# Decoder layer on one core: two weight sums by adding transfers, four pairs in six gate blocks, and seven products for the last 1024 columns

## The chip, the cores and the metric

The kernel runs on one core of one Trainium2 chip. The metric is the device time of one execution in microseconds. Before the change the median of 3 runs is 1021.54 us (1021.4 to 1021.66).

## What is computed

One layer for 256 tokens of width 2048 in float32: a wide input projection, two token mixers (attention and a short gated convolution), two gates computed from the input, and an output projection.

```python
h = _rmsnorm(x, pre_norm_g)
proj = jnp.einsum('bsd,de->bse', h, w_in)
...
attn = attn.reshape(b, s, MLA_WIDTH) * jax.nn.silu(z_mla)
y_mla = jnp.einsum('bse,ed->bsd', attn, w_o_mla)
u = c_gate * c_in
...
y_conv = jnp.einsum('bse,ed->bsd', b_gate * conv * jax.nn.silu(z_conv), w_o_conv)
merged = jax.nn.sigmoid(g_mla) * y_mla + jax.nn.sigmoid(g_conv) * y_conv
out = jnp.einsum('bsd,de->bse', merged, w_out)
x = x + _rmsnorm(out, post_norm_g)
```

The change concerns the products with 2048 x 1024 pieces of `w_in` (z_conv, b_gate, g_mla, g_conv) and of `w_out`.

## The kernel before

**Split numbers.** Every float32 operand becomes two parts of a shorter format, high and low. For a weight, ACT writes the high part (`whi`, a copy that rounds) and DVE subtracts it from the original (`wlo`). One `product` (L90 is its matmul) is then three matmuls of a 128x128 stationary tile of tokens with 512 weight columns: high by high, high by low, low by high.

**Units.** Weights come in 192 units, numbered in load order, most of them 128x2048 floats (1 MiB). `load_raw` issues each on the queue of SP into one of three `raw` buffers; `split_unit` makes `whi` and `wlo` in rings of three. `take(i)` calls `ahead`, which writes the loads three units and the splits one unit further down the program than the matmuls that use them. Matmuls are kept in program order, as is what is marked `keep_in_program_order`; a scheduler places the rest, each engine runs its own list in order, and semaphores join the lists.

**Blocks.** From about 419 us on the kernel works through eight gate blocks (`block(n, ...)`, 1024 columns each: units 81 to 88, 89 to 96, and so on to 137 to 144), then 32 units of two square products (the stage `sq`, 145 to 176), then a block with the first 1024 columns of the output projection (177 to 184, named `OUT`), then its last 1024 columns as eight units (185 to 192). A block has eight units of 256 input rows and fills eight PSUM banks. A **whole** unit gives 24 matmuls to the banks 2, 3, 4, 0. A **pair** is a unit whose two row groups and two column halves are multiplied as a 2x2 matrix product with seven products instead of eight (21 matmuls), into the banks 7, 5, 1, 6, 4, 2, 3 in this order. It needs sums of the token tiles, made once by `token_sums` (`xs`), and sums of the four column blocks of the unit: `split_pair` makes them on DVE in three steps, blocks 1 and 2 less block 0 into `tf` (1024 columns), one into block 0's place in `raw`, one into `tf`; then the parts `thi` (ACT) and `tlo` (DVE). `tf`, `thi` and `tlo` exist once. `PLACES` says which units of a block are pairs: 2 and 4 in block 0, 0, 2 and 4 in the blocks 1 to 7, 3 and 5 in `OUT`; the rest are whole.

**The end of a block.** After its last pair ACT copies bank 1 to `p1` and DVE makes three sums `u` from the banks 6, 7 and 5; that frees the banks 1, 6, 7, 5 for the next block. Behind the last unit `done` adds one of `p1`, `u` to each of the banks 2, 3, 4, 0. For gates the sum goes to a tile `sg` and through a sigmoid, and POOL's queue stores it to memory; stage `sq` loads it again. For the output, `out_block` squares the result on ACT, multiplies it by the norm's gain into `og`, and `finish` scales it, adds the residual `xr` and stores it.

**The last columns.** The third 512 columns (four units) go through the bank pair `cv`; of the last 512 the four units' parts are kept, so that the first half of the tokens is through and being normalised while the second half is multiplied. `xr`, 2 MB, is loaded on ACT's queue when that stage begins.

Of the kernel before, what the change touches and what calls it, by code (L numbers as in the profile page):

```python
# [84 lines left out]
def tile_layer(ctx: ExitStack, tc: tile.TileContext, xw, x, pos, pvec, post_g, wc, wz, wcv, wkr, wqk, wqr, wv, cwr, wsq, wg, out):  # L85
# [61 lines left out]

    u_g.append([add(wg[OUT, i], kind=kinds[OUT][i][0]) for i in range(KD // 2)])
    u_out = {(c, k): add(wsq[2, c, k], kind="whole") for c in (2, 3) for k in range(4)}

    raws, splits, early = {}, {}, {}
    done = {"raw": 0, "split": 0}

    def load_raw(i):
        ap, w, _ = plan[i]
# [3 lines left out]
        cuts = {0: (S, XW, 2 * XW), 1: (0, XW, 2 * XW), 2: (0, XW, 2 * XW)}.get(i, (0, w))  # L159
# [10 lines left out]
    def split_unit(i):  # L170
# [28 lines left out]
        for h in range(0, w, n):  # L199
            e = min(h + n, w)  # L200
            split_act(hi[:, h:e], lo[:, h:e], t[:, h:e])
        splits[i] = hi, lo

    tpool = {}

    def split_pair(i, t, hi, lo):

        raw = t[:, :].rearrange("p (b c) -> p b c", b=4)
        tf = tpool["f"].tile([P, 2, 3, S], F32, name=f"tf{i}", tag="tf", bufs=1)[:, :, :, :].rearrange("p a b c -> p (a b c)")
        tf = tf.rearrange("p (b c) -> p b c", b=3)  # L210
        thi, tlo = (tpool["t"].tile([P, 3, 512], F32R, name=f"t{o}{i}", tag=f"t{o}", bufs=1) for o in ("hi", "lo"))
# [4 lines left out]
        nc.scalar.activation(hi[:, 512:], t[:, 512:], AF.Copy)  # L216
        tt(tf[:, :2], raw[:, 1:3], raw[:, 0:1].to_broadcast([P, 2, 512]), op=ALU.subtract)
        tt(raw[:, 0], raw[:, 2], tf[:, 0], op=ALU.add)
        tt(tf[:, 2], raw[:, 3], raw[:, 0], op=ALU.subtract)
        nc.scalar.activation(hi[:, :512], t[:, :512], AF.Copy)  # L220
        nc.scalar.activation(thi[:, :, :], tf[:, :, :], AF.Copy)  # L221
# [93 lines left out]
    at_f = fp.tile([P, H, S], F32, name="at_f")  # L315
    cv_f = fp.tile([P, KD, S], F32, name="cv_f")
# [469 lines left out]
    def token_sums(pool, pairs):  # L786
# [14 lines left out]
        tt(a22, a21, a22, op=ALU.add)  # L801
# [3 lines left out]
        tt(a12, a12, a11, op=ALU.subtract)  # L805
# [31 lines left out]
    for h in range(H):  # L837
# [21 lines left out]
        if h == H - 3:  # L859
            lstack.close()  # L860
            tpool["f"] = dstack.enter_context(tc.tile_pool(name="d0", bufs=1))
            sums = token_sums(tpool["f"], PAIRS)
            next(sums)
# [42 lines left out]
    def side(n, j):  # L906

        i = {5: 0, 6: 1, 7: 2, 3: 3}.get(n)
        if i is not None:
            return [tpool["xs"][:, i, j, h] for h in range(2)]  # L910
# [8 lines left out]
    def block(n, done, jobs):  # L919
# [42 lines left out]
        for m, t, half, other in ((2, 0, 0, p1[:, :]), (3, 0, 1, u[:, 0]), (4, 1, 0, u[:, 2]), (0, 1, 1, u[:, 1])):  # L962
            done(ps[m][:, :], other, t, half)

# [3 lines left out]
    def open_spool():  # L968
        bstack.close()
        spool["pool"] = main.enter_context(tc.tile_pool(name="sp", bufs=1, side="right"))  # L970
        spool["pool"].tile([P, 512], F32, name="sg_first", tag="sg", bufs=4)
        spool["w"] = wstack.enter_context(tc.tile_pool(name="cw", bufs=1, side="right")).tile([P, NT, D], F32, name="cv_w")
# [12 lines left out]
    gate_far = {}  # L985

    def g_done(n, b):
        def done(ps, other, t, half):
            c = 2 * b + half
            g = spool["pool"].tile([P, 512], F32, name=f"sg{n}{c}{t}", tag="sg", bufs=4)  # L990
            nc.vector.tensor_tensor(g[:, :], ps, other, op=ALU.add)
# [305 lines left out]
```

## Time and profile before

| what | value |
|---|---|
| median of 3 runs | 1021.54 us |
| profiled execution | 1021.4 us |
| its span in the trace | 1019.6 us |
| gate blocks, from the first to the last matmul | 419 to 752 us |
| stage `sq` | 752 to 926 us |
| block `OUT` | 926 to 968 us |
| last 1024 columns | 968 to 1011.7 us |
| traffic to and from memory | 240.46 MB, mean 236 GB/s |
| matmuls in the program | 4608 |

The span runs from the first to the last instruction of the trace; 1.8 us of the profiled execution lie around it. PE is the matrix engine and PEld its loading of stationary tiles, DVE and ACT the two engines that split, POOL and SP issue transfers. The four stages of the table are told apart by the names of the tiles that the matmuls write and read.

### The profile page before, as it was taken

The numbers are of one execution on the slowest core, as the hardware profiler recorded it, in microseconds if no ns is written. First come the engines' busy times: TensorE is split into PE (matmuls) and PEld (weight loads), VectorE is DVE, ScalarE is ACT, GpSimd is POOL, SyncE is SP. The second block draws the span as 40 slices with busy tenths as digits, with TensorE's granted clock in tenths as the row PEclk, the third lists the DMA queues.
The fourth block names the chain that finished last, engine by engine and source line by source line (L and its number), as shares of the span: only waits on it lengthen the run. The fifth ranks groups of instructions, "written<-read, shape, count | busy, mean of one in ns | idle before, by whom it ended". The sixth has DMA issues, their size and how long they took to land.

```text
span 1019.6 us, 12601 instructions
## 1 busy us (share of the span) xinstructions
PE 1010.1 (99%) x4619; PEld 842.3 (83%) x4619; DVE 798.5 (78%) x1010; ACT 547.0 (54%) x682; POOL 199.8 (20%) x381
## 2 busy tenths in 40 slices
PE   9999999999999999999999999999999999999996
PEld 7888888888888888888888888888888888888885
DVE  7578787887869777888989889898878875678762
ACT  7756555565566664655545456555653443344551
POOL 7530311232213223200000000000024431322000
PEclk9999999999999999999999999999999999999999
DMA  8755785786666656665566566665679896778662
GB/s 324 301 193 195 229 258 184 216 282 234 218 225 219 244 191 232 218 221 212 176 223 237 213 236 240 213 247 216 238 254 329 312 338 216 267 257 283 214 242 82
DMA packets 44830, 240.46 MB, mean 236 GB/s; under 512 B 8096, under 2 KB 8800, under 8 KB 21856
## 3 DMA queue, kind: packets, MB, share of 16 engines
q1 hardware_dynamic: 29808, 197.54, 54.6%
q0 software_dynamic: 14528, 38.82, 11.7%
q10 hardware_dynamic: 432, 3.29, 0.9%
q8 instruction: 36, 0.59, 0.2%
q14 instruction: 26, 0.21, 0.1%
HBM read 217.63 MB, written 17.83 MB: 231 GB/s over the span
## 4 chain that ended last, share of the span: by engine, by line
PE 98%; DMA 1%; DVE 0%; ACT 0%; SPq 0%; DVEq 0%; issue 0%
PE g L90 37%; PE cv L90 26%; PE sq L90 17%; PE out L90 4%; PE kn L90 2%; PE qn L90 2%; PE vv L90 2%; PE ckv L90 2%; PE qa L90 2%; PE sc L90 1%; PE qr L90 1%; PE o L90 1%; DMA raw<-xw_dram 1%; PE kr L90 0%; DVE og L1149 0%; SPq L161 0%
## 5 line engine op out<-in xcount | busy, mean ns | idle before, releaser
L273 DVE TENSOR_TENSOR wlo<-raw,whi 128x1024 fp32r<-128x1024 f32 (+2 forms) x233 | 363.7, 1578 | 124.5 <-ACT whi L272 123.6
L272 ACT ACTIVATE whi<-raw 128x1024 fp32r<-128x1024 f32 (+2 forms) x235 | 307.2, 1334 | 251.7 <-PE sq L90 85.2
L90 PE MATMUL g<-whi,x_both 128*128 128x512 f32 x852 | 275.0, 389 | 0.0
L90 PE MATMUL cv<-whi,x_both 128*128 128x512 f32 x768 | 242.9, 390 | 0.0
L90 PEld LDWEIGHTS g<-whi,x_both 128*128 128x128 f32 x852 | 159.9, 188 | 33.3
L90 PEld LDWEIGHTS cv<-whi,x_both 128*128 128x128 f32 x768 | 144.2, 188 | 29.3
L90 PE MATMUL g<-wlo,x_both 128*128 128x512 f32 x426 | 165.7, 389 | 0.0
L90 PE MATMUL cv<-wlo,x_both 128*128 128x512 f32 x384 | 149.7, 390 | 0.0
L359 POOL DMA_DIRECT2D far<-via x96 | 52.6, 554 | 231.1 <-DVE via L352 229.2
L90 PEld LDWEIGHTS g<-wlo,x_both 128*128 128x128 f32 x426 | 80.0, 188 | 16.5
L90 PEld LDWEIGHTS cv<-wlo,x_both 128*128 128x128 f32 x384 | 72.2, 188 | 13.9
L216 ACT ACTIVATE whi<-raw 128x1536 fp32r<-128x1536 f32 x25 | 37.3, 1491 | 80.1 <-PE g L90 49.3
L90 PE MATMUL sq<-whi,x_both 128*128 128x512 f32 x256 | 79.0, 389 | 0.0
L90 PE MATMUL sq<-whi,cv_both 128*128 128x512 f32 x256 | 79.0, 389 | 0.0
L214 DVE TENSOR_TENSOR wlo<-raw,whi 128x2048 fp32r<-128x2048 f32 x25 | 57.2, 2290 | 8.1 <-ACT whi L220 8.1
L90 PEld LDWEIGHTS sq<-whi,x_both 128*128 128x128 f32 x256 | 48.0, 188 | 9.9
L90 PEld LDWEIGHTS sq<-whi,cv_both 128*128 128x128 f32 x256 | 48.0, 188 | 9.9
L90 PE MATMUL sq<-wlo,x_both 128*128 128x512 f32 x128 | 49.8, 389 | 0.0
L90 PE MATMUL sq<-wlo,cv_both 128*128 128x512 f32 x128 | 49.8, 389 | 0.0
L214 DVE TENSOR_TENSOR tf<-raw 128x1024 f32<-128x1024 f32 (+1 forms) x50 | 47.7, 954 | 0.8
L214 DVE TENSOR_TENSOR tlo<-tf,thi 128x1536 fp32r<-128x1536 f32 x25 | 43.8, 1753 | 2.3 <-ACT thi L221 2.3
L221 ACT ACTIVATE thi<-tf 128x1536 fp32r<-128x1536 f32 x25 | 37.1, 1484 | 10.7 <-PE g L90 9.3
(248 smaller groups left out, 1389.9 us busy)
## 6 DMA issues: line engine op xcount, KB each, us to landing
raw<-wg_dram SPq DMA_DIRECT2D x72, 1024.0 KB, 4.8
raw<-wsq_dram SPq DMA_DIRECT2D x40, 1024.0 KB, 6.1
raw<-wcv_dram SPq DMA_DIRECT2D x32, 1024.0 KB, 4.9
raw<-wz_dram SPq DMA_DIRECT2D x16, 1024.0 KB, 4.9
raw<-wqk_dram SPq DMA_DIRECT2D x8, 1024.0 KB, 5.1
raw<-wc_dram SPq DMA_DIRECT2D x4, 1024.0 KB, 10.0
raw<-wv_dram SPq DMA_DIRECT2D x4, 1024.0 KB, 4.8
gate<-sg POOLq DMA_DIRECT2D x16, 256.0 KB, 2.6
```

Of the source, the lines that this page charges most:

```text
L90: return tc.keep_in_program_order(nc.tensor.matmul(*a, **kw))
L214: tc.keep_in_program_order(nc.vector.tensor_tensor(*a, op=op))
L216: nc.scalar.activation(hi[:, 512:], t[:, 512:], AF.Copy)
L221: nc.scalar.activation(thi[:, :, :], tf[:, :, :], AF.Copy)
L272: a = nc.scalar.activation(hi, src, AF.Copy)
L273: b = nc.vector.tensor_tensor(lo, src, hi.bitcast(F32), op=ALU.subtract)
L359: tc.keep_in_program_order(nc.gpsimd.dma_start(out=f[i], in_=m))
```

## The change

1. **Sums by addition.** The two differences in `split_pair` become sums; the signs move into `token_sums` and into the last steps of `u`.
2. **Two sums by transfer.** For the pairs from unit 93 to the end of block 7 the first two sums no longer run on DVE. A transfer on POOL's queue writes column block 0 into two places of `tf`, and a second one, with an adding write, adds the blocks 1 and 2. The unit's own load leaves out its first 512 columns, which DVE then fills with the third sum as before.
3. **Doubled buffers.** `tf`, `thi` and `tlo` alternate between two places (the pools `d0` and `d2`; the second `tf` lies in the place of `u`).
4. **Four pairs** (units 0, 2, 4, 6) in the blocks 1 to 6. `extra_sums`, in block 1, makes the token sums of the fourth. One whole unit is left behind the last pair instead of three. `u` and `p1` lie in the four `sg` tiles, the gates are made in place, and their stores go to SP's queue, at the third unit of the next block (`store`). `ahead(..., split=2)` at a block's last pair and last unit brings splits one unit further forward.
5. **The last 1024 columns as a block** (`OUT + 1`) with pairs at the units 1 and 3. Its last three units are kept (`KEPT`) and used bank by bank (`last_units`); the sum for the last bank is split into two parts (`more`) and added by two matmuls with an identity matrix (`one`). `out_block` of `OUT` moves to the third unit of this block, and `xr` goes into the place of `cv_f`, which is free earlier.

The program has 4586 matmuls.

```diff
-    u_g.append([add(wg[OUT, i], kind=kinds[OUT][i][0]) for i in range(KD // 2)])
-    u_out = {(c, k): add(wsq[2, c, k], kind="whole") for c in (2, 3) for k in range(4)}
+    u_g += [[add(wg[n, i], kind=kinds[n][i][0]) for i in range(KD // 2)] for n in (OUT, OUT + 1)]
+    FIRST_SUM = u_g[1][4]
...
-        ap, w, _ = plan[i]
+        ap, w, kind = plan[i]
+        by_dma = kind == "pair" and FIRST_SUM <= i <= u_g[OUT - 1][-1]
+        if by_dma:
+            sums_by_dma(i, ap)
...
-        cuts = {0: (S, XW, 2 * XW), 1: (0, XW, 2 * XW), 2: (0, XW, 2 * XW)}.get(i, (0, w))
+        cuts = {0: (S, XW, 2 * XW), 1: (0, XW, 2 * XW), 2: (0, XW, 2 * XW)}.get(i, (512 if by_dma else 0, w))
...
-        if u_out[3, 0] <= i < u_out[3, 3]:
-            hi, lo = (op2.tile([P, UNIT], F32R, name=f"w{o}{i}") for o in ("hi", "lo"))
+        if i == u_g[-1][-1]:
+            both = fp.tile([P, 2, UNIT], F32R, name="w_kept", tag="at_f", bufs=1)
+            hi, lo = both[:, 0], both[:, 1]
...
+    def sum_tile(i):
+        second = "t2" in tpool and tpool["n"] % 2
+        tpool["n"] += 1
+        if second:
+            return tpool["t"].tile([P, 3, 512], F32, name=f"tf{i}", tag="u", bufs=1)[:, :, :], True
+        tf = tpool["f"].tile([P, 2, 3, S], F32, name=f"tf{i}", tag="tf", bufs=1)[:, :, :, :].rearrange("p a b c -> p (a b c)")
+        return tf.rearrange("p (b c) -> p b c", b=3), False
+    def sums_by_dma(i, ap):
+        tf, _ = sums_come[i] = sum_tile(i)
+        keep = tc.keep_in_program_order
+        keep(nc.gpsimd.dma_start(out=tf[:, :2], in_=ap[:, :512].rearrange("p (a c) -> p a c", a=1).to_broadcast([P, 2, 512])))
+        keep(nc.gpsimd.dma_start(out=tf[:, :2], in_=ap[:, 512:1536].rearrange("p (a c) -> p a c", a=2), accum_op=ALU.add))
...
-        tf = tpool["f"].tile([P, 2, 3, S], F32, name=f"tf{i}", tag="tf", bufs=1)[:, :, :, :].rearrange("p a b c -> p (a b c)")
-        tf = tf.rearrange("p (b c) -> p b c", b=3)
-        thi, tlo = (tpool["t"].tile([P, 3, 512], F32R, name=f"t{o}{i}", tag=f"t{o}", bufs=1) for o in ("hi", "lo"))
+        tf, second = sums_come.get(i) or sum_tile(i)
+        thi, tlo = (tpool["t2" if second else "t"].tile([P, 3, 512], F32R, name=f"t{o}{i}", tag=f"t{o}", bufs=1) for o in ("hi", "lo"))
...
+        if i not in sums_come:
+            tt(tf[:, :2], raw[:, 1:3], raw[:, 0:1].to_broadcast([P, 2, 512]), op=ALU.add)
         tt(raw[:, 0], raw[:, 2], tf[:, 0], op=ALU.add)
-        tt(tf[:, 2], raw[:, 3], raw[:, 0], op=ALU.subtract)
-        nc.scalar.activation(hi[:, :512], t[:, :512], AF.Copy)
-        nc.scalar.activation(thi[:, :, :], tf[:, :, :], AF.Copy)
+        tt(tf[:, 2], raw[:, 3], raw[:, 0], op=ALU.add)
+        rounded(hi[:, :512], t[:, :512])
+        rounded(thi[:, :, :], tf[:, :, :])
...
-        tt(a22, a21, a22, op=ALU.add)
+        tt(a22, a21, a22, op=ALU.subtract)
         tt(a21, a11, a21, op=ALU.subtract)
         yield
         tt(a11, a22, a11, op=ALU.subtract)
-        tt(a12, a12, a11, op=ALU.subtract)
+        tt(a12, a12, a11, op=ALU.add)
...
+            if i == len(kinds) - kept:
+                return last_units(ps, units[i:], kinds[i:], w, u, p1)
...
-                p1 = wide("p1")
-                u = tpool["t"].tile([P, 3, 512], F32, name="u", tag="u", bufs=1)
-                nc.scalar.activation(p1[:, :], ps[1][:, :], AF.Copy)
-                tt = nc.vector.tensor_tensor
-                tt(u[:, 0], ps[6][:, :], p1[:, :], op=ALU.add)
-                tt(u[:, 2], ps[7][:, :], u[:, 0], op=ALU.add)
+                if i > 5:
+                    ahead(units[i], split=2)
+                if 0 < n < OUT:
+                    p1, *u = (spool["pool"].tile([P, 512], F32, name=f"u{n}{o}", tag="sg", bufs=4)[:, :] for o in range(4))
+                else:
+                    p1, u = wide("p1")[:, :], tpool["t"].tile([P, 3, 512], F32, name="u", tag="u", bufs=1)
+                    u = [u[:, o] for o in range(3)]
+                nc.scalar.activation(p1, ps[1][:, :], AF.Copy)
+                def tt(*a, op):
+                    r = nc.vector.tensor_tensor(*a, op=op)
+                    if last_pair > 5:
+                        tc.keep_in_program_order(r)
+                tt(u[0], ps[6][:, :], p1, op=ALU.add)
+                tt(u[2], ps[7][:, :], u[0], op=ALU.add)
                 for o in (1, 0):
-                    tt(u[:, o], u[:, 2 * o], ps[5][:, :], op=ALU.subtract)
+                    tt(u[o], ps[5][:, :], u[2 * o], op=ALU.subtract)
+        if n < OUT - 1:
+            ahead(units[-1], split=2)
+        for m, t, half, other in ((2, 0, 0, p1), (3, 0, 1, u[0]), (4, 1, 0, u[2]), (0, 1, 1, u[1])):
             done(ps[m][:, :], other, t, half)
+    def last_units(ps, units, kinds, w, u, p1):
+        ws = [w]
+        pool = out_tiles["pool"]
+        one, more = pool.tile([P, P], F32R, name="one"), pool.tile([P, 2, 512], F32R, name="more")
+        nc.scalar.activation(one[:, :], ident[:, :], AF.Copy)
+        for t, banks in enumerate((((2, p1), (3, u[0])), ((4, u[2]), (0, u[1])))):
+            for half, (m, other) in enumerate(banks):
+                if m == 0:
+                    for a in range(2):
+                        matmul(ps[m][:, :], one[:, :], more[:, a], start=False, stop=False)
+                for i, (_, ks) in enumerate(kinds):
+                    if i == len(ws):
+                        ws.append(take(units[i]))
+                    for j, k in enumerate(ks):
+                        a = [x_both[:, k, o + t * P : o + (t + 1) * P] for o in (0, S)]
+                        product(ps[m][:, :], a, ws[i](2 * j + half, 512), False, i == len(kinds) - 1 and j == 1)
+                if t == 0 == half:
+                    split_act(more[:, 0], more[:, 1], u[1], True)
+                out = ps[m][:, :]
+                if t == 0 or half == 0:
+                    nc.vector.tensor_tensor(other, out, other, op=ALU.add)
+                    out = other
+                rr = out_block(2 + half, t, out)
+            finish(t, rr)
+    def extra_sums():
+        hi = tpool["t2"].tile([P, 4, P], F32R, name="xs4hi")
+        lo = tpool["t"].tile([P, 512], F32R, name="xs4lo", tag="p1", bufs=1)[:, :].rearrange("p (i t) -> p i t", i=4)
+        xf = spool["pool"].tile([P, 512], F32, name="xf4", tag="sg", bufs=4)[:, :].rearrange("p (g s) -> p g s", g=2)
+        tpool["xs4"] = hi, lo
...
+            tt(xf[:, g], a[:, 3 + STEP * g, :S], a[:, 3 + STEP * g, S:], op=ALU.add)
+        (a11, a21), (a12, a22) = [[xf[:, g, t * P : (t + 1) * P] for t in range(NT)] for g in range(2)]
+        tt(a22, a21, a22, op=ALU.subtract)
+        tt(a21, a11, a21, op=ALU.subtract)
+        tt(a11, a22, a11, op=ALU.subtract)
+        tt(a12, a12, a11, op=ALU.add)
+        for i, f in enumerate((a22, a11, a21, a12)):
+            split_act(hi[:, i], lo[:, i], f, True)
...
+    def store():
+        while stores:
+            stores.pop(0)()
...
-            tc.keep_in_program_order(nc.gpsimd.dma_start(out=gate_far[n, c, t][:, :], in_=g[:, :]))
+            far = gate_far[n, c, t]
+            stores.append(lambda: nc.sync.dma_start(out=far[:, :], in_=g))
...
+        jobs = {2: [extra_sums]} if n == 0 else {2: [store]}
+    store()
     split_branch(3)
...
+        out_later.append(lambda: out_block(half, t, other))
...
-    block(OUT, out_done, {3: [open_out]})
-    main.close()
-    op2 = ctx.enter_context(tc.tile_pool(name="op2", bufs=1))
-    xr, og = op2.tile([P, NT, D], F32, name="xr"), out_tiles["og"]
-    nc.scalar.dma_start(out=xr[:, :, :], in_=x)
-    pss = [bank(f"out2_{t}", tag="cv", bufs=2) for t in range(NT)]
-    for kk in range(4):
-        out_products(pss, take(u_out[2, kk]), kk)
-    for t in range(NT):
-        out_block(2, t, pss[t][:, :])
-    nc.vector.reduce_sum(part[:, :], ssq[:, :, :3], axis=mybir.AxisListType.X)
-    nc.vector.tensor_scalar(part[:, :], part[:, :], 1.0 / D, EPS, op0=ALU.mult, op1=ALU.add)
-    pss = [bank(f"out3_{t}") for t in range(NT)]
-    for t in range(NT):
-        for kk in range(4):
-            if t == 0:
-                last.append(take(u_out[3, kk]))
-            out_product(pss[t], t, last[kk], kk)
-        finish(t, out_block(3, t, pss[t][:, :]))
+    block(OUT, out_done, {3: [open_out], 8: [lambda: ahead(u_g[OUT + 1][0])]})
+    xr = fp.tile([P, KD, S], F32, name="xr", tag="cv_f", bufs=1)[:, :, :].rearrange("p k s -> p (k s)")
+    xr, og = xr.rearrange("p (t d) -> p t d", t=NT), out_tiles["og"]
+    nc.scalar.dma_start(out=xr, in_=x)
+    block(OUT + 1, None, {2: out_later}, KEPT)
...
+KEPT = 3
-PLACES = [(2, 4)] + [(0, 2, 4)] * 7 + [(3, 5)]
+PLACES = [(2, 4)] + [(0, 2, 4, 6)] * 6 + [(0, 2, 4)] + [(3, 5), (1, 3)]
```

Two places in the instruction lists (a row is the line, the operation, out<-in and the size; the number behind a name is the unit or the block with its bank, then a running number).

DVE before, where block 4 (units 113 to 120) gives way to block 5 (121 on):

```order
L273 TENSOR_TENSOR wlo119_5449<-raw119_5412,whi119_5448 128x2048
L956 TENSOR_TENSOR u_5440<-g4_6_5275,p1_5439 128x512
L957 TENSOR_TENSOR u_5440<-g4_7_5272,u_5440 128x512
L959 TENSOR_TENSOR u_5440<-u_5440,g4_5_5273 128x512 x2
L273 TENSOR_TENSOR wlo120_5479<-raw120_5446,whi120_5478 128x2048
L214 TENSOR_TENSOR tf121_5510<-raw121_5476 128x1024
L214 TENSOR_TENSOR raw121_5476<-raw121_5476,tf121_5510 128x512
L214 TENSOR_TENSOR tf121_5510<-raw121_5476 128x512
L214 TENSOR_TENSOR wlo121_5509<-raw121_5476,whi121_5508 128x2048
L214 TENSOR_TENSOR tlo121_5512<-tf121_5510,thi121_5511 128x1536
L991 TENSOR_TENSOR sg000_5545<-g4_2_5276,p1_5439 128x512
L273 TENSOR_TENSOR wlo122_5576<-raw122_5506,whi122_5575 128x2048
```

After, the same place:

```order
L299 TENSOR_TENSOR wlo120_5534<-raw120_5491,whi120_5533 128x2048
L234 TENSOR_TENSOR raw121_5531<-raw121_5531,tf121_5528 128x512
L234 TENSOR_TENSOR tf121_5528<-raw121_5531 128x512
L234 TENSOR_TENSOR wlo121_5559<-raw121_5531,whi121_5558 128x2048
L234 TENSOR_TENSOR tlo121_5561<-tf121_5528,thi121_5560 128x1536
L989 TENSOR_TENSOR u41_5570<-g4_6_5322,u40_5569 128x512
L989 TENSOR_TENSOR u43_5572<-g4_7_5319,u41_5570 128x512
L1083 TENSOR_TENSOR u40_5569<-g4_2_5323,u40_5569 128x512
L989 TENSOR_TENSOR u42_5571<-g4_5_5320,u43_5572 128x512
L989 TENSOR_TENSOR u41_5570<-g4_5_5320,u41_5570 128x512
L299 TENSOR_TENSOR wlo122_5605<-raw122_5578,whi122_5604 128x2048
L1083 TENSOR_TENSOR u43_5572<-g4_4_5325,u43_5572 128x512
```

Before, the four `u` of block 4 stand between the splits of the units 119 and 120, and unit 121's sums begin with the 1024 columns of `tf`. After, that row is gone, the `u` (now `u40` to `u43`) stand behind the whole first pair of the next block, and one of the gate sums (L1083) is among them.

POOL before, the stores of the gates of block 4 and the first of block 5:

```order
L995 DMA gate000_5548<-sg000_5545 128x512
L995 DMA gate010_5553<-sg010_5550 128x512
L995 DMA gate001_5558<-sg001_5555 128x512
L995 DMA gate011_5563<-sg011_5560 128x512
L995 DMA gate020_5841<-sg020_5838 128x512
```

After, at the same place of the program, for the units 117 to 121:

```order
L224 DMA tf117_5394<-wg_dram 128x2x512
L225 DMA tf117_5394<-wg_dram 128x1024
L224 DMA tf119_5461<-wg_dram 128x2x512
L225 DMA tf119_5461<-wg_dram 128x1024
L224 DMA tf121_5528<-wg_dram 128x2x512
L225 DMA tf121_5528<-wg_dram 128x1024
```

The stores are gone from POOL; a plain and an adding transfer for each pair have come.

More of the change, by code (lines that the diff above doesn't have):

```diff
@@ L861, in tile_layer @@
             tpool["f"] = dstack.enter_context(tc.tile_pool(name="d0", bufs=1))
-            sums = token_sums(tpool["f"], PAIRS)
+            sums = token_sums(tpool["f"], 3)
             next(sums)
@@ L909, in side @@
         if i is not None:
-            return [tpool["xs"][:, i, j, h] for h in range(2)]
+            return [tpool["xs"][:, i, j, h] for h in range(2)] if j < 3 else [tpool["xs4"][h][:, i] for h in range(2)]
         k, t = {1: (j, 0), 2: (j + STEP, 0), 4: (j + STEP, 1)}[n]
@@ L917, in tile_layer, with block @@
     TAGS = {7: ("cv", 2), 5: ("cv", 2), 1: ("st", 1), 6: ("o", 1), 4: ("mm", 4), 2: ("mm", 4), 3: ("mm", 4), 0: ("mm", 4)}
-    def block(n, done, jobs):
+    def block(n, done, jobs, kept=0):
         units, kinds = u_g[n], gate_kinds()[n]
@@ new lines, in extra_sums, with tt @@
+    def extra_sums():
[3 more added lines that the diff above has]
+        tpool["xs4"] = hi, lo
+        a = x_both[:, :, :].bitcast(F32)
+        def tt(*a, op):
+            tc.keep_in_program_order(nc.vector.tensor_tensor(*a, op=op))
+        for g in range(2):
+            tt(xf[:, g], a[:, 3 + STEP * g, :S], a[:, 3 + STEP * g, S:], op=ALU.add)
[6 more added lines that the diff above has]
+            split_act(hi[:, i], lo[:, i], f, True)
@@ L983, in zc_done @@
         return done
-    gate_far = {}
+    gate_far, stores = {}, []
+    def store():
+        while stores:
+            stores.pop(0)()
     def g_done(n, b):
@@ L1082, in tile_layer @@
     tpool.update(f=dd, t=dd)
+    del tpool["t2"]
     waiting = None
@@ L1124, in out_done @@
         nc.vector.tensor_tensor(other, ps, other, op=ALU.add)
-        out_block(half, t, other)
+        out_later.append(lambda: out_block(half, t, other))
     def out_block(c, t, ps):
@@ L1132, in out_block @@
         og_now = nc.vector.tensor_tensor(og[:, t, cs], ps, gb[:, cs], op=ALU.mult)
+        if c == 2:
+            p = part[:, t : t + 1]
+            nc.vector.reduce_sum(p, ssq[:, t, :3], axis=mybir.AxisListType.X)
+            nc.vector.tensor_scalar(p, p, 1.0 / D, EPS, op0=ALU.mult, op1=ALU.add)
         if c == 3:
@@ L1135, in out_block @@
             return row_norm(t)
-    last = []
     def row_norm(t):
@@ L1276 @@
             w.reshape(4, 4, P, 4, 512).transpose(3, 0, 2, 1, 4).reshape(4, 4, P, UNIT)
-            for w in (w_o_mla, w_o_conv, w_out)
+            for w in (w_o_mla, w_o_conv)
         ]),
```

33 lines of the change are left out of this document (18 added, 15 removed).

## The prediction

> **What bounds the kernel now.** I read the chain of waits first, then the busy table, the groups of instructions by shape, the stretches by stage and the transfers.
>
> ```profile
> 424.83 327.12 PE g L90 x1443
> 751.95 174.08 PE sq L90 x768
> 926.03 42.16 PE g L90 x186
> 968.19 43.53 PE out L90 x192
> ...
> 1011.75 0.70 ACT junk L1131 x2
> ```
>
> These are pieces of the chain that ended last, in order of time: start, length, what. From 424.83 to the last matmul at 1011.7 us there is nothing but PE, and one piece begins where the other ends. In the pieces whose records are complete a matmul of 512 columns takes 43.53/192 = 42.16/186 = 174.08/768 = 0.2267 us (the 1443 of the first piece are too few; some records are missing). The 389 ns in the groups is the length of one pipelined matmul, not its price. So time is matmuls times 0.2267 us as long as nothing starves PE; the end behind them is 1019.6 - 1011.7 = 7.9 us.
>
> ```profile
> span 1019.6 us, 12601 instructions
> ...
> PE 1010.1 (99%) x4619; PEld 842.3 (83%) x4619; DVE 798.5 (78%) x1010; ACT 547.0 (54%) x682; POOL 199.8 (20%) x381
> ```
>
> The profiled execution took 1021.4 us, 1.8 more than its span; the median of the runs is 1021.54. Next to PE stands DVE, and in the stage that the change touches it has less room than 78% says:
>
> ```profile
> 418.80:460.40 41.60, 41.60 (x187) 34.47 (x186) 36.58 (x33) 24.25 (x20) 5.44 (x10) 1.00 0.63 225
> ...
> 544.40:585.90 41.50, 41.50 (x185) 34.37 (x184) 35.71 (x29) 20.48 (x15) 2.16 (x4) 1.00 0.64 228
> 752.00:839.00 87.00, 87.00 (x385) 72.05 (x384) 68.76 (x68) 37.63 (x29) 39.02 (x72) 1.00 0.92 324
> 968.20:1011.70 43.50, 43.50 (x192) 35.68 (x191) 21.77 (x23) 16.77 (x20) 0.00 (x0) 1.00 0.43 168
> ```
>
> Stretches: length, busy time of PE, PEld, DVE, ACT, POOL, the granted clock, DMA share, GB/s. A gate block (second row) holds 35.71 us of DVE work in 41.5; PE is never short, at clock 1.00. In the third row PE runs unbroken at 324 GB/s and a DMA share of 0.92.
>
> **The matmuls.** A pair of units costs 7 products of 3 matmuls, 21; two products more for a whole unit's four banks make 24. Six blocks get one more pair: 6 x 3 = 18 matmuls fewer. The last 1024 columns' second half had 8 whole units, 192; now 2 pairs and 6 wholes, 42 + 144 = 186, and 2 that add the saved sum into a bank: 188, 4 fewer. Together 22 x 0.2267 = **4.99 us**, all on the path if what follows stays hidden.
>
> **Room on DVE and ACT.**
>
> ```profile
> L273 DVE TENSOR_TENSOR wlo<-raw,whi 128x2048 fp32r<-128x2048 f32 x87 | 198.9, 2287 | 77.4 <-ACT whi L272 76.8
> ...
> L214 DVE TENSOR_TENSOR wlo<-raw,whi 128x2048 fp32r<-128x2048 f32 x25 | 57.2, 2290 | 8.1 <-ACT whi L220 8.1
> ...
> L214 DVE TENSOR_TENSOR tlo<-tf,thi 128x1536 fp32r<-128x1536 f32 x25 | 43.8, 1753 | 2.3 <-ACT thi L221 2.3
> ...
> L216 ACT ACTIVATE whi<-raw 128x1536 fp32r<-128x1536 f32 x25 | 37.3, 1491 | 80.1 <-PE g L90 49.3 <-issue 27.4 <-PE cv L90 3.4
> L221 ACT ACTIVATE thi<-tf 128x1536 fp32r<-128x1536 f32 x25 | 37.1, 1484 | 10.7 <-PE g L90 9.3 <-ACT whi L220 0.9 <-DVE tf L214 0.3
> ...
> L214 DVE TENSOR_TENSOR tf<-raw 128x1024 f32<-128x1024 f32 x25 | 30.4, 1216 | 0.0
> ...
> L214 DVE TENSOR_TENSOR tf<-raw 128x512 f32<-128x512 f32 x25 | 17.3, 691 | 0.8
> L214 DVE TENSOR_TENSOR raw<-raw,tf 128x512 f32<-128x512 f32 x25 | 17.2, 686 | 0.5
> ...
> L220 ACT ACTIVATE whi<-raw 128x512 fp32r<-128x512 f32 x25 | 15.6, 623 | 4.9 <-DVE raw L214 4.9
> ...
> L991 DVE TENSOR_TENSOR sg<-g,u 128x512 f32<-128x512 f32 x12 | 7.6, 682 | 0.0
> ```
>
> A pair now costs DVE 1.22 + 0.69 + 0.69 + 2.29 + 1.75 = 6.64 us, a whole unit 2.29. With its first two sums brought by transfers a pair costs 5.42. One block: one pair for a whole, +3.13; three pairs lose 1.22 each, -3.66. DVE goes from 35.7 to 35.2 us while PE goes from 183 to 180 matmuls, 40.80 us: as full as before. ACT gains 1.49 + 0.62 + 1.48 - 1.9 = 1.7 in 20.5 to 24.3. The second block is the tight one: two of its pairs still sum on DVE (+2.4), and the token sums for the fourth pair add ten small instructions, at most 0.42 each (the row below), 4.2. That is 41.8 us in 40.8; the first block's spare 5.0 us (36.58 in 41.60) hides it, and without that cover it is 1.0 us, once.
>
> ```profile
> 906.63 0.42 DVE L794 TENSOR_TENSOR xf<-xf 128x256 f32<-128x256 f32 x1
> ```
>
> **The change of blocks.** Before, three whole units lay behind a block's last pair, 16.3 us in which banks 7, 5, 1 and 6 were emptied. Now one does, 5.44 us. Let T be the start of that pair on PE. The buffer of the next block's first pair is free at T; ACT rounds its parts until T+2.1 (1.49 + 0.62) and T+3.6, then takes bank 1. DVE: `wlo` 2.29 to T+4.4, `tlo` 1.75 to T+6.2, five instructions of 0.68 (four `u`, one store sum) to T+9.6, the next whole unit to T+11.9, bank 4 to T+12.6. PE starts the next block at T+4.76+5.44 = T+10.2, asks for bank 5 at T+10.9 and for bank 4 (after 12 matmuls) at T+12.9. Slack 1.3 and 0.3 us, and more by the rows below: DVE's next instruction begins 2.21 us after a 2.29 one, 0.07 less than its length, over eight of them 0.6. I cost it at nothing; were it late by 0.5, six changes cost 3.0.
>
> ```profile
> 577.23 2.29 DVE L214 TENSOR_TENSOR wlo<-raw,whi 128x2048 fp32r<-128x2048 f32 x1 [0.52 <-ACT whi L220]
> 579.44 1.75 DVE L214 TENSOR_TENSOR tlo<-tf,thi 128x1536 fp32r<-128x1536 f32 x1
> ```
>
> **The sums that come by transfer.** The new wait: DVE's `raw` instruction of a pair waits for a plain and then an adding transfer on POOL, 0.5 MiB each, one after the other; behind it on DVE stand all further splits, and PE waits for those. Two buffers take turns, so each serves every second pair: half a block, 20.40 us. From arrival to release it needs 0.69 + 0.69 + 2.29 + 1.75 = 5.4 us (ACT's roundings lie beside). So the chain of two transfers may last 20.4 - 5.4 = **15.0 us**. No row shows an adding transfer; the nearest:
>
> ```profile
> raw<-wg_dram SPq DMA_DIRECT2D x72, 1024.0 KB, 4.8
> ...
> gate<-sg POOLq DMA_DIRECT2D x16, 256.0 KB, 2.6
> gs<-gate POOLq DMA_DIRECT2D x16, 256.0 KB, 5.5
> ...
> raw<-wsq_dram SPq DMA_DIRECT2D x16, 1024.0 KB, 7.6
> gs<-gate POOLq DMA_DIRECT2D x10, 256.0 KB, 6.7
> ...
> cw<-cwr_dram POOLq DMA_DIRECT2D x3, 256.0 KB, 10.4
> ```
>
> The first three are of the whole run, the others of 752 to 839 us; the last figure is microseconds to landing. A block moves 228 GB/s x 41.5 = 9.5 MB; each DMA-summed pair adds 1 MiB and saves a quarter, +3.1 MB: 12.6 MB in 40.8, 309 GB/s, less than the 324 under which PE ran unbroken. At 228 GB/s 256 KB and 1 MB land in 5.5 and 4.8, at 324 in 6.7 and 7.6; 309 lies at 0.84 of the way, 6.8 us each, **13.6** for the two: slack 1.4. The ends: 2 x 2.6 = 5.2, and 2 x 10.4 = 20.8, which costs (20.8 - 15.0) x 12 half blocks = 70 us. I take 13.6, from the rows nearest in size and rate.
>
> The stores of the gates leave POOL for SP, between loads; they are issued two units into the next block, when the sigmoids are done, and the raw loads behind them have until the third unit after. Free.
>
> **The last columns.** DVE works 21.77 of 43.5 us; two pairs add 4.35 each and the bank sums 4.8: 35 of 42.6. Three kept units are used whole for one bank before the next, so all are split early. Let Z be the start of the last pair. DVE can sum from Z + 2.7 (12 matmuls); four sums of 0.68 and three splits of 2.29 take 9.6, to Z+12.4. PE asks for the third unit's `wlo` after that pair, one whole unit and 12 matmuls, at Z + 4.76 + 5.44 + 2.72 + 0.23 = Z+13.15: slack 0.7. The load of `xr`, 2 MB, moves ahead into a stage at 250 GB/s. The end stays 7.9. Sum: 1021.4 - 4.99 = 1016.4; on the median, **1016.5**.
>
> **Rivals.** (1) The change of blocks isn't cleared in time: 0.3 to 0.8 us six times; at 0.5, 1019.5. For: slack 0.3 before the overlap; against: the overlap.
> (2) The chain of sums is the longer loop. It decides from 15.0 us, and from 15.4 (5.0/12) it is slower than before. If both land in 7.6 and are issued in 0.55 each it is 16.3: 12 x 1.3 = 15.6, 1032. For: the 10.4 row, and the two transfers meet raw loads. Against: they are half as large.
> (3) The transfers fill the engines, if an addition reads its destination too: 4 x 0.52 MB more, 14.7 MB a block.
>
> ```profile
> q1 hardware_dynamic: 1160, 8.45, 57.9%
> ...
> GB/s 140 281 398 355 394 187 47 250 429 273 125 335 414 140 0 140 304 414 140 62 187 421 328 0 0 148 445 390 16 78 234 437 250 0 78 187 429 304 250 62
> ```
>
> In the 42 us from 544 on, loads moved 8.45 MB in 57.9% of the time, 347 GB/s. At that rate 14.7 MB take 42.4 us, 1.6 over, six times: 9.4 us, 1025.9. Against it: single slices reach 420 to 445 GB/s, at which they take 34. The Trainium skill states the mechanism ("Collectives: The Full Stack", section "The bandwidth ceiling: the fold count and why AG ≠ RS ≠ AR"): an adding transfer is slower not for the addition but because it reads two sources, which halves the rate; by it the sum would be (3)'s, with plain reading (3) falls away, and no run here shows which.
> (4) Fewer matmuls don't shorten it because something else set the pace: 1021.4. The unbroken PE pieces speak against it.
>
> **Numbers.** Forecast 0.62, (1) 0.14, (2) 0.16, (3) 0.05, (4) 0.03. About 0.2%, 2 us, is what a measurement of this kernel can tell from no change. Faster: forecast and half of (1), 0.69. Same: the other half and (4), 0.10. Slower: (2) and (3), 0.21. Range: 1015.8 to 1026 takes in all but (2); the forecast alone 1015.8 to 1017.5.
>
> **What would show it.** In the profile after: PE unbroken from 424.8, its pieces 22 matmuls shorter; DVE some 35 us a block; the POOL transfers landing in 6 to 7.5 us; DVE's wait for them short. Wrong: `g` matmuls that wait for `thi` or `tlo` of a pair (2), for the first matmuls of a block (1), or raw loads landing far above 7.6 us (3).

## The result, and the profile after

The changed kernel takes 1047.76 us (median of 5 runs, 1047.25 to 1052.89) against 1021.4 us before, measured beside it: a ratio of 1.0269, 95% interval 1.0256 to 1.0282. It is 26 us slower where 5 us faster was forecast, and lies above the whole range. The profiled execution took 1047.25 us, its span 1045.4.

Where the time went is read from the chain of work that ended last (start, length, what), of the changed kernel:

```profile
424.93 76.22 PE g L90 x336
...
524.56 8.96 issue
533.54 8.32 DMA tf<-wg_dram
...
571.74 9.46 issue
582.82 10.09 issue
594.53 7.78 issue
602.33 10.66 DMA tf<-wg_dram
...
737.53 41.21 PE g L90 x180
778.74 174.08 PE sq L90 x768
952.82 84.79 PE g L90 x374
```

Before, this chain was one PE piece after another. Now it leaves PE at 501 us and comes back to it for good at 737.5; between them it runs over the `tf` transfers (the long "issue" pieces are POOL waiting for a plain transfer to land) and DVE's splits. From the first long piece to stage `sq` it takes 778.74 - 424.93 = 353.8 us; before it took 327.1, and the 18 matmuls fewer should have made it 323.0. So 30.8 us are lost in the gate blocks. Everything else came as forecast: `sq` 174.08 as before, the output 84.79 us where the same matmuls took 42.16 + 43.53 = 85.69 (4 matmuls of 0.2267 fewer), and 1045.4 - 1037.6 = 7.8 us behind them.

The waits of the changed kernel (who waits for what: us in total, times, longest):

```profile
POOL tf L225 <- DMA tf<-wg_dram: 203.5, 25, 10.2
...
POOL tf L224 <- DVE tlo L234: 42.5, 15, 6.8
```

```profile
DVE raw L234 <- DMA tf<-wg_dram: 61.1, 17, 8.9
```

DVE's `raw` instruction, the one that takes the sums from the transfers, waits 61 us in all for them. PE's own waits in the gate blocks show under another name:

```profile
PE g L90 <- DVE u L989: 17.3, 11, 5.3
PE g L90 <- DVE tlo L234: 2.3, 2, 1.7
```

Most of them are at the change of blocks, for a bank that a `u` sum has to free. By the signs that the prediction lists that would be its rival (1). But `u` stands on DVE behind the whole first pair of the next block, and so behind the wait for that pair's transfers; the run with one transfer, below, has the same change of blocks and no wait there.

The landings of the plain (L224) and the adding transfers (L225) between 480 and 730 us:

```profile
L224 POOL DMA_DIRECT2D tf<-wg_dram x22: 727/727/1049, 482.0 to 724.0; - x22
...
DMA to landing us min/median/max: 5.9/9.1/10.8
```

```profile
L225 POOL DMA_DIRECT2D tf<-wg_dram x21: 870/876/893, 490.9 to 723.5; - x21
...
DMA to landing us min/median/max: 5.2/7.3/10.7
```

A landing is counted from the start of the issue. The two last 9.1 + 7.3 = 16.4 us (a sum of medians); 13.6 was forecast, with 15.0 as the limit. And POOL's own timeline (start, length, what, the idle time before it) shows a second thing:

```profile
570.12 0.88 POOL L225 DMA_DIRECT2D tf<-wg_dram  x1 [9.28 <-DMA tf<-wg_dram]
570.70 1.04 POOL L224 DMA_DIRECT2D tf<-wg_dram  x1
581.21 0.87 POOL L225 DMA_DIRECT2D tf<-wg_dram  x1 [9.47 <-DMA tf<-wg_dram]
581.79 1.02 POOL L224 DMA_DIRECT2D tf<-wg_dram  x1
592.92 0.88 POOL L225 DMA_DIRECT2D tf<-wg_dram  x1 [10.11 <-DMA tf<-wg_dram]
```

The plain transfer of the next pair (L224) stands on POOL behind the adding one of this pair (L225), which waits until its own plain one has landed. Here POOL issues a pair every 11 to 12 us where PE needs one every 10.2. Of the 25 plain transfers 15 waited for DVE and one, the first, for PE (24.8 us); the other 9 stood behind an adding one.

### The profile page after: what moved, and what is told of

Its sections match the earlier page's. It is cut to its first block, busy times and chain, and to the rows that moved or that the text cites. A ratio compares the mean times of both kernels' runs of the same rounds, so it can differ in the third digit from the quotient of the medians.

```text
span 1045.4 us, 12701 instructions
## 1 busy us (share of the span) xinstructions
PE 1016.2 (97%) x4597; PEld 841.3 (80%) x4597; DVE 809.4 (77%) x1037; ACT 562.5 (54%) x705; POOL 227.2 (22%) x407
## 3 DMA queue, kind: packets, MB, share of 16 engines
q0 software_dynamic: 19808, 58.75, 20.9%
## 4 chain that ended last, share of the span: by engine, by line
PE 76%; issue 11%; DVE 6%; DMA 5%; POOL 1%; ACT 0%; SPq 0%; DVEq 0%; POOLq 0%
PE cv L90 25%; PE g L90 20%; PE sq L90 17%; DMA tf<-wg_dram 4%; PE kn L90 2%; PE qn L90 2%; PE vv L90 2%; PE ckv L90 2%; DVE tlo L234 2%; PE qa L90 2%; DVE wlo L234 2%; PE sc L90 1%; PE qr L90 1%; PE o L90 1%; DVE u L989 1%
## 5 line engine op out<-in xcount | busy, mean ns | idle before, releaser
L299 DVE TENSOR_TENSOR wlo<-raw,whi 128x1024 fp32r<-128x1024 f32 (+2 forms) x224 | 343.2, 1550 | 99.6 <-ACT whi L298 98.9
L298 ACT ACTIVATE whi<-raw 128x1024 fp32r<-128x1024 f32 (+2 forms) x226 | 289.9, 1310 | 194.0 <-PE sq L90 84.2
L90 PE MATMUL g<-whi,x_both 128*128 128x512 f32 x868 | 286.5, 391 | 0.0
L237 ACT ACTIVATE whi<-raw 128x1536 fp32r<-128x1536 f32 x66 | 69.7, 1059 | 139.2 <-DVE raw L234 74.4
L90 PEld LDWEIGHTS g<-wlo,x_both 128*128 128x128 f32 x434 | 82.1, 189 | 17.1
L234 DVE TENSOR_TENSOR wlo<-raw,whi 128x2048 fp32r<-128x2048 f32 x33 | 75.6, 2291 | 1.3 <-ACT whi L237 1.2
L234 DVE TENSOR_TENSOR raw<-raw,tf 128x512 f32<-128x512 f32 x33 | 22.8, 690 | 61.3 <-DMA tf<-wg_dram 61.1
L225 POOL DMA_DIRECT2D tf<-wg_dram x25 | 21.9, 878 | 203.5 <-DMA tf<-wg_dram 203.5
L90 PE MATMUL g<-thi,xs 128*128 128x512 f32 x108 | 42.2, 422 | 17.4 <-DVE u L989 17.3
L234 DVE TENSOR_TENSOR tlo<-tf,thi 128x1536 fp32r<-128x1536 f32 x33 | 57.8, 1752 | 0.0
L237 ACT ACTIVATE thi<-tf 128x1536 fp32r<-128x1536 f32 x33 | 49.2, 1491 | 4.2 <-ACT whi L237 0.9
```

What stands on the lines that cost most here:

```text
L90: return tc.keep_in_program_order(nc.tensor.matmul(*a, **kw))
L225: keep(nc.gpsimd.dma_start(out=tf[:, :2], in_=ap[:, 512:1536].rearrange("p (a c) -> p a c", a=2), accum_op=ALU.add))
L234: tc.keep_in_program_order(nc.vector.tensor_tensor(*a, op=op))
L237: r = nc.scalar.activation(*a, AF.Copy)
L298: a = nc.scalar.activation(hi, src, AF.Copy)
L299: b = nc.vector.tensor_tensor(lo, src, hi.bitcast(F32), op=ALU.subtract)
```

## The experiments

All are edits of the changed kernel, three rounds each beside the kernel before (medians of 1021.39 to 1021.63 us).

### Sums on DVE again

```diff
-        by_dma = kind == "pair" and FIRST_SUM <= i <= u_g[OUT - 1][-1]
+        by_dma = False
```

> All weight sums made on DVE again, everything else as changed. Theory A (the two transfers are a chain that is longer than the loop of two buffers): the 31 us lost in the gate blocks go away, and DVE, with 35.2 + 4 x 1.22 = 40.1 us of work in a block of 40.8, sets what is left: 1016.5 to 1024. Theory B (the transfers fill the DMA engines): the same, 1016.5 to 1024. Theory C (four pairs leave too little room at the change of blocks, whoever makes the sums): above 1030.

Measured: 1019.88 us, ratio 0.9981 (0.9972 to 0.9990). The 28 us that it lies below the changed kernel come from the transfers, not from four pairs or the change of blocks: theory C falls. What is left above 1016.5 fits DVE: in each gate block the chain of this run goes over DVE's splits and sums for 17.5 us before it is back on PE, a block takes 41.24 us in place of 40.80, and DVE is nearly full, as a window shows (length, then busy time of PE, PEld, DVE, ACT, POOL, the clock, DMA share, GB/s):

```profile
586.00:628.00 42.00, 41.87 (x185) 34.37 (x184) 40.22 (x33) 25.09 (x20) 0.00 (x0) 1.00 0.67 226
```

That is 40.2 us of DVE work in 42.

### The second transfer plain, and one transfer alone

```diff
-        keep(... in_=ap[:, 512:1536] ..., accum_op=ALU.add))
+        keep(... in_=ap[:, 512:1536] ...))
```

> The second transfer of a pair writes plainly in place of adding (the addition is left out, so the first two weight sums lack column block 0); the same two transfers, waits and bytes from memory. Theory A: the chain keeps its two landings, the second by a little shorter, 1040 to 1048. Theory B with the price in the addition (it reads its destination): the second lands in half its time, the software queue's share falls from 20.9% to about 16%, 1020 to 1035. Theory C: 1047.

Measured: 1016.93 us, ratio 0.9958 (0.9944 to 0.9971). Then the first transfer was taken out too:

```diff
-        keep(nc.gpsimd.dma_start(out=tf[:, :2], in_=ap[:, :512]...to_broadcast([P, 2, 512])))
```

> The first transfer of a pair is left out and the second writes plainly (the first two weight sums lack column block 0): one landing in the chain, half the added bytes. Theory A: the chain is about 9 us, under 15.0, so 1016.5 to 1018. Theory B: 19 us of DMA work a block less 10, 1016.5 to 1020. Theory C: above 1030.

Measured: 1016.19 us, ratio 0.9944 (0.9927 to 0.9960).

So the addition alone is worth 1047.76 - 1016.93 = 30.8 us: two transfers of the same bytes, in the same order, with the same waits, cost 0.7 us more than one. With one transfer PE runs unbroken; in its chain:

```profile
424.49 323.04 PE g L90 x1425
747.53 174.08 PE sq L90 x768
921.61 84.79 PE g L90 x374
```

323.04 is 327.12 - 18 x 0.2267 to the hundredth. With two plain ones the first and the second landed, between 480 and 730 us, in:

```profile
DMA to landing us min/median/max: 4.1/7.5/9.7
```

```profile
DMA to landing us min/median/max: 3.4/5.8/8.8
```

7.5 + 5.8 = 13.3 us, under the limit of 15.0, but with little to spare: from 510 to 707 us the chain of this kernel, too, runs over the transfers, though PE hardly idles. Theory A's 1040 falls, since two landings at plain prices fit. Theory B's second form is right in that the price lies in the addition. Its numbers weren't: 1016.93 lies below its 1020, the queue's share fell to 18.2% and not to 16%, and the second landing went from 7.3 to 5.8 us and not to half.

What the addition does to the engines, in windows over the same 210 us, the changed kernel first, then the one with two plain transfers:

```profile
502.00:712.00 210.00, 191.62 (x801) 153.84 (x800) 160.37 (x131) 108.38 (x90) 28.03 (x35) 0.96 0.87 269
```

```profile
502.00:712.00 210.00, 209.91 (x926) 173.35 (x926) 178.67 (x146) 123.61 (x103) 25.84 (x41) 1.00 0.87 302
```

At the same DMA share of 0.87 the kernel that adds moves 269 GB/s, the other 302. The first row also shows longer matmuls: 191.62/801 = 0.239 us each against 0.2267, at a granted clock of 0.96. That makes 10 of the 28 us by which PE is behind in this window; the other 18 it stands idle. As the chain does not touch PE between 501 and 737.5 us, the slower matmuls seem to fill time in which PE would have waited; no run separates the two.

The software queue's packets tell the price; for the kernels with all sums on DVE, one transfer, two plain, and plain and adding:

```profile
q0 software_dynamic: 12608, 32.53, 10.1%
```

```profile
q0 software_dynamic: 16208, 45.64, 13.5%
```

```profile
q0 software_dynamic: 19808, 58.75, 18.2%
```

```profile
q0 software_dynamic: 19808, 58.75, 20.9%
```

The bytes of the last two are equal; reading the destination isn't counted in them. As time of 16 engines: 0.101 x 1018.0 = 102.8 us, 0.135 x 1014.2 = 136.9, 0.182 x 1014.9 = 184.7, 0.209 x 1045.4 = 218.5. For each of 25 pairs the transfer of the blocks 1 and 2 costs (136.9 - 102.8)/25 = 1.36 us when plain, and the addition (218.5 - 184.7)/25 = 1.35 more. (These are rough: the kernel with half loads, below, makes the same transfers as the changed one, and its 21.1% of 1023.9 us is 216.0.) The Trainium skill ("Collectives: The Full Stack", section "The bandwidth ceiling: the fold count and why AG ≠ RS ≠ AR") says of a collective's ReduceScatter that it is slow because its add needs two source reads, at about half the rate. Taken over to this transfer the rule gives twice a plain one's time; here 2.71 against 1.36 agrees; with a broadcast source, further down, it was less.

### Transfers for two pairs of a block, or for one

```diff
-        by_dma = kind == "pair" and FIRST_SUM <= i <= u_g[OUT - 1][-1]
+        by_dma = kind == "pair" and FIRST_SUM <= i <= u_g[OUT - 1][-1] and (i - u_g[1][0]) % 4 == 0
```

> Only the units 0 and 4 of each block get their sums by transfers, the units 2 and 6 on DVE; nothing is left out. DVE has 35.2 + 2.4 = 37.6 us a block. Each transferred pair still has 15.0 us for its two transfers, but they no longer stand behind the other pair's on POOL. Theory A: at 16.7 us a chain (9.9 + 6.8 as measured) 12 half blocks lose some 1.7 each, 1037; if the landings shorten to 13 together, 1016.5 to 1018. Theory B: half the added work, DMA no longer full, 1016.5 to 1018. Theory C: above 1030.

Measured: 1017.45 us, ratio 0.9958 (0.9943 to 0.9973). Then for one pair:

```diff
-        ... and (i - u_g[1][0]) % 4 == 0
+        ... and (i - u_g[1][0]) % 8 == 2
```

> Only unit 2 of each block gets its sums by transfers, the other pairs on DVE; nothing is left out. DVE has 35.2 + 3.66 = 38.9 us in 40.8, and unit 2's sums are the ones that stood in the chain where all sums ran on DVE. All theories: 1016.2 to 1018; above 1019 if DVE's change of blocks is still the limit.

Measured: 1017.16 us, ratio 0.9957 (0.9940 to 0.9974). Both beat both kernels; between them there is no difference to be told. In the second, PE is unbroken from 500 us to the end of the blocks:

```profile
499.85 248.65 PE g L90 x1097
```

with 39.6 us of DVE work in a window of 42 and a DMA share of 0.76:

```profile
586.00:628.00 42.00, 42.00 (x187) 34.76 (x187) 39.56 (x34) 25.11 (x22) 1.61 (x2) 1.00 0.76 246
```

### The engines or the chain: less traffic, more traffic, other roles

Whether an adding transfer hurts because it is long in the chain or because it fills the engines for all others was asked three times. First less traffic beside it:

```diff
-        cuts = {...}.get(i, (512 if by_dma else 0, w))
+        cuts = {...}.get(i, (512 if by_dma else HALF if FIRST_SUM <= i <= u_g[OUT - 1][-1] else 0, w))
...
+            split_act(two[0], two[1], two[2][:, 1:2].to_broadcast([P, 2, HALF]), True)
```

> The change as it is, adding transfers and all, but of every whole unit from unit 93 to the end of block 7 only the second half is loaded, and split twice (the products with the first half's weights are left out). Loads fall by 2.1 MB a block of 12.6, nothing in the chain of two transfers or on DVE, ACT and PE changes. Theory D (the addition costs time of the DMA engines, and full engines make all landings late): landings shorten, 1016 to 1024. Theory E (the adding transfer is slow by itself, whatever else runs): 1035 to 1047.

Measured: 1025.45 us, ratio 1.0038 (1.0023 to 1.0053): 22.3 of the 30.8 us are gone, 8.5 remain. Just outside D's span, far from E's: most is the load of the engines, not all. It is the plain landing that got shorter, 6.5 us (median, same stretch) in place of 9.1; the adding one stayed at 7.3. Then more traffic beside two plain transfers:

```diff
-        keep(... in_=ap[:, 512:1536] ..., accum_op=ALU.add))
+        keep(... in_=ap[:, 512:1536] ...))
+        away = dram.tile([P, HALF], F32, name=f"away{i}", tag=f"away{i}", bufs=1)
+        keep(nc.gpsimd.dma_start(out=away[:, :], in_=ap[:, 512:1536]))
```

> The second transfer writes plainly (the addition is left out, as in the run with two plain transfers, 1016.93), and behind it POOL issues one more plain transfer of 0.5 MiB from the same weights to a scratch place in memory, for which nothing waits. It gives the DMA engines about the work that the addition was measured to take (1.35 us of all 16 engines for each pair), but adds nothing to the chain except an issue. Theory D: most of the loss returns, 1035 to 1048. Theory E: 1017 to 1024.

Measured: 1034.06 us, ratio 1.0122 (1.0107 to 1.0137): a transfer that nobody waits for brings back 17.1 us. Between the two spans, nearer to D. With the roles of the two transfers swapped:

```diff
-        keep(... in_=ap[:, :512]...to_broadcast([P, 2, 512])))
-        keep(... in_=ap[:, 512:1536] ..., accum_op=ALU.add))
+        keep(... in_=ap[:, 512:1536] ...))
+        keep(... in_=ap[:, :512]...to_broadcast([P, 2, 512]), accum_op=ALU.add))
```

> The two transfers change roles: column blocks 1 and 2 are written plainly, then block 0 is added in two places; the sums are the same. Theory D: the addition doubles the dearer of the two (1.91 us of the engines against 1.36), so 0.5 us more work for each pair, 1048 to 1060. Theory E: the same two landings in another order, 1040 to 1050.

Measured: 1053.42 us, ratio 1.0316 (1.0288 to 1.0345), in D's span. Its trace doesn't show D's sum, though. The software queue took 20.2% of 1049.2 us, 211.9, which is less than the 218.5 before the swap. By the same count the broadcast transfer costs (184.7 - 136.9)/25 = 1.91 us of all engines when plain and (211.9 - 136.9)/25 = 3.00 when it adds, 1.6 times and not twice. What grew is the second landing, 8.9 us (median) against 7.3. Why it grew stays open.

### A shorter chain with the same traffic

```diff
-        keep(... in_=ap[:, :512]...to_broadcast([P, 2, 512])))
-        keep(... in_=ap[:, 512:1536] ..., accum_op=ALU.add))
+        for b in range(2):
+            keep(nc.gpsimd.dma_start(out=tf[:, b], in_=ap[:, :512]))
+        for b in range(2):
+            keep(nc.gpsimd.dma_start(out=tf[:, b], in_=ap[:, 512 * b + 512 : 512 * b + 1024], accum_op=ALU.add))
```

> The change as it is, but each of the two transfers of a pair is issued as two of 512 columns: two plain ones, then two adding ones, so that the first addition starts when half of the plain data has landed. Same bytes, same sums, two more issues on POOL for each pair (0.7 us each). Theory F (PE waits for the chain of two landings, which the engines' load only stretches): the chain is shorter by some 2 us of the 2.6 that each half block is late, 1020 to 1036. Theory G (the DMA engines' time alone decides): as before, 1044 to 1052.

Measured: 1037.41 us, ratio 1.0166 (1.0146 to 1.0185), just above theory F's span and far below G's. In the next one the halves are undone and the plain transfer goes to SP:

```diff
-        keep(nc.gpsimd.dma_start(out=tf[:, :2], in_=ap[:, :512]...to_broadcast([P, 2, 512])))
+        nc.sync.dma_start(out=tf[:, :2], in_=ap[:, :512]...to_broadcast([P, 2, 512]))
```

> The plain transfer of each pair is issued by SP, ahead of the unit's load, and only the adding one by POOL, so that no plain transfer waits for the adding one of the pair before it; bytes, sums and buffers are the same. In 10 of the 25 pairs of the changed kernel the plain transfer was issued right behind an adding one. Theory F with the queue's order as part of the chain: those pairs gain 1 to 2 us each, 1030 to 1040. Theory F with the buffers alone, and theory G: 1044 to 1050.

Measured: 1038.37 us, ratio 1.0181 (1.0158 to 1.0205). Each takes away some 10 us: the chain and the order on POOL's queue count, theory G falls. The Trainium skill ("DMA: Bandwidth & Descriptors", section "Issuing engines are not separate DMA queues") says that issuing from more engines saves only the usually small time of issuing. Here it saved 9.4 us. Part of that is the issue itself, which takes 0.73 to 1.05 us on POOL and 0.38 on SP. Part is the queue: in the blocks 3 to 6 a plain issue came 0.75 us (mean of 16) after DVE had freed its buffer in the changed kernel, and 0.03 us after it here. The engines are fuller then; the window of the kernel with the plain transfers on SP:

```profile
502.00:712.00 210.00, 199.80 (x856) 162.00 (x855) 162.90 (x135) 110.83 (x92) 16.40 (x19) 0.98 0.94 282
```

0.94 in place of 0.87. That suggested a floor by full engines, and two last runs asked for it: both shortenings together, and less traffic (the edit of `cuts` above) together with SP. The first, over the kernel in halves:

```diff
         for b in range(2):
-            keep(nc.gpsimd.dma_start(out=tf[:, b], in_=ap[:, :512]))
+            nc.sync.dma_start(out=tf[:, b], in_=ap[:, :512])
```

> Both shortenings of the chain at once: each transfer in two of 512 columns, the plain ones issued by SP, the adding ones by POOL; bytes, sums and buffers as in the change. Each of the two alone gave 1037 to 1038 at a DMA share of 0.92 to 0.99 in most stretches. Theory H (behind the chain the full DMA engines are the next bound, with some 41.7 us of work a block of 40.8): no further gain, 1034 to 1039. Theory I (only the chain decides, and the two gains of 10 us add): 1026 to 1031.

Measured: 1030.18 us, ratio 1.0079 (1.0056 to 1.0103); its six runs spread from 1026.3 to 1034.0. Theory I's span: the gains nearly add (9.4 + 10.4 = 19.8 expected, 17.6 measured), and no floor shows at 1037. The second:

> Both reliefs at once: half of every whole unit's load left out as before (alone 1025.45), and the plain transfers issued by SP (alone 1038.37). Theory H: with the engines no longer full and the queue out of the chain the loss is gone, 1016 to 1018.5. Theory I, or another cause besides these two: above 1020.

Measured: 1017.01 us, ratio 0.9963 (0.9953 to 0.9974). Theory H's span: with less traffic and the queue out of the way the loss is gone, though every pair still has its plain and its adding transfer one behind the other. So neither the full engines nor the order alone is the cause. The plain landing lengthens with what else is on the engines, and the chain of landings is what PE, by way of DVE, waits for; a change in either moves the time. The DMA share by itself doesn't tell it: this kernel has 0.87 from 502 to 712 us, as the changed one. How much the engines alone would cost under a chain that never waits stays open.

## Why the prediction was wrong

**The matmuls: right.** 323.04 us for the gate blocks and 84.79 for the output are the forecast's 18 and 4 fewer; with one transfer the kernel takes 1016.19, and 1016.5 was forecast. (The prediction calls the 1443 matmuls of the first piece too few; 1443 x 0.2267 = 327.1 is the whole of it.)

**DVE and ACT: right.** In the windows of that kernel DVE works 36.0 us in 42, 35.0 in a block of 40.8; 35.2 was forecast. ACT works 22.3 to 25.6 us there, with 22.2 to 26.0 forecast. The tight second block starved nobody: from 461 to 500 us PE is busy all 39 us in the changed kernel too. With all sums on DVE 40.1 us a block was expected; 40.2 in 42 is 39.5 in a block of 41.24.

**The change of blocks: put at nothing, rightly.** With one transfer PE doesn't wait there. The waits for `u` in the changed kernel come from the late sums, and rival (1) falls.

**Stores on SP, the last columns, `xr`, the end: put at nothing, rightly**, by the same unbroken chain.

**The sums that come by transfer: wrong.** The step that failed is "I take 13.6, from the rows nearest in size and rate". Those rows were all of plain transfers, and for two plain transfers 13.3 us is what came. That it came so close is in part luck: the 5.5 us "at 228 GB/s" is the median of 16 `gs` loads that all start between 756 and 896 us, in stage `sq`, so no row gave a load of 256 KB at 228. The addition made it 16.4, over the limit of 15.0.

The limit was itself too wide, as it left nothing for the steps between. A buffer's round through two pairs, from the starts and landings in the trace (means of the 16 pairs of the blocks 3 to 6), has in the changed kernel 9.29 us for the plain landing, 0.33 to the adding issue, 7.44 for its landing, 0.41 until DVE takes it, 5.36 on DVE and 0.75 to the next plain issue: 23.6 where PE's pace is 20.4. With two plain transfers the same six are 7.30, 0.29, 6.18, 0.95, 5.36 and 0.55, 20.6. So the limit lay nearer 20.4 - 5.36 - 0.29 - 0.02 - 0.29 = 14.4 (the steps without any wait), and the plain chain already filled its loop. Eight rounds of 3.2 us too much make 25 of the 30.8 us in these four blocks.

The prediction had the reason in rival (3), where the read of the destination doubles the transfer, and gave it 0.05: "single slices reach 420 to 445 GB/s, at which they take 34". A slice of that view is 1 us. Over 210 us no run moved more than 329 GB/s (the one with the extra plain transfer, at a share of 0.93), and the adding ones 269 at 0.87 and 282 at 0.94, not counting the read of the destination.

**The size of the rivals.** Rival (2) had the place right, but its price was worked out with the landings independent of rival (3). By the measured 16.4 it gives (16.4 - 15.0) x 12 = 17 us; the rest is the steps between. One of them is POOL's queue: the plain transfer of the next pair was counted as free to start with its buffer, but in 9 of 25 pairs it stood behind the adding one. Issuing it from SP was worth 9.4 us. (2) and (3) were priced as two cases that exclude each other; they are one, with (3) stretching (2).

## What to carry to other kernels

Cost an adding transfer well above a plain one of its size (here 2.0 and 1.6 times the engines' time), and put its load on every other landing, not on its own alone. When a spare engine takes work off a full one, take as much as makes room and no more: one or two pairs of four were enough here, and all four were some 30 us slower than that. When a loop of transfers has a limit, count the time from each landing to the next issue too. Look at what an issue waits behind on its queue: here a transfer whose issue waited for a landing held up the next plain one. And where PE waits need not be where the time is lost: here it waited for `u`, and the cause was a transfer for which the splits ahead of `u` waited.

## What the runs showed of the hardware

- An adding transfer of 0.5 MiB cost the DMA engines about twice a plain one (2.71 against 1.36 us of all 16 engines), with a broadcast source 1.6 times (3.00 against 1.91). The profile's bytes don't show it: 58.75 MB on POOL's queue with and without the addition, at shares of 20.9% and 18.2%.
- Landings grew long before the DMA share was full, and the share alone doesn't fix them. The plain transfer took 4.6 us (median, 480 to 730 us) in the kernel that used transfers for two pairs of four, 7.5 with two plain transfers a pair, 9.1 with the adding ones, at shares of 0.77 to 0.86, 0.82 to 0.90 and 0.86 to 0.88. Issued from SP with half of the whole units' loads left out it took 5.7, at 0.83 to 0.90.
- From a landing to the issue on POOL that waited for it 0.29 us passed (0.44 at times), to DVE's instruction 0.02.
- The kernels scatter unequally: 1026.3 to 1034.0 us with both shortenings and 1051.0 to 1057.7 with the roles swapped, but 1033.1 to 1034.8 with the extra transfer and 1017.04 to 1017.20 with transfers for a single pair. What decides it isn't shown.
